# Seven products for the convolution gate zc, and a layer norm one pair sooner

## The chip, the cores and the metric

The kernel runs on one core of a Trainium2 chip. The metric is the device time of one execution in microseconds (us); lower is better. A run's time is that of its only core.

The engines: TensorE (PE) multiplies; PEld is its weight load; VectorE (DVE), ScalarE (ACT) and GpSimd (POOL) do elementwise work; SyncE (SP) issues DMA transfers. ACT and POOL issue some DMAs too. SBUF is the on-chip memory (128 partitions), PSUM holds matmul results, DRAM is the memory outside.

## The reference

One decoder layer on x of 512 tokens x 2048 channels, in float32. One combined projection by w_in (2048 x 7168) gives seven parts of 1024 columns; eight heads of 128 run causal stick-breaking attention, and a depthwise convolution of width 31 with layer norm and a pointwise product makes the other half.

```python
h = _rmsnorm(x, g_pre)
q, k, v, z_att, u, g_glu, z_conv = jnp.split(h @ w_in, IN_SPLITS, axis=-1)
y_att = _stick_breaking_attention(q, k, v) * jax.nn.silu(z_att)
# _conformer_conv: u * sigmoid(g_glu), causal conv (31 taps) + conv_b,
#                  layernorm over channels, silu, then @ w_pw2 + b_pw2
y_conv = _conformer_conv(u, g_glu, ...) * jax.nn.silu(z_conv)
y = jnp.concatenate([y_att, y_conv], axis=-1) @ w_out
x = x + _rmsnorm(y, g_post)
```

The part the change concerns is `z_conv`, called zc in the kernel: 512 x 2048 times 2048 x 1024, then silu, then a product with the pointwise output.

## The kernel before

**Arithmetic.** Each float32 operand is split in two parts, hi (rounded by ACT, line 99) and lo (the rest, subtracted by DVE, line 100), and each product is three matmuls: hi·hi, hi·lo, lo·hi (`mm3`, lines 342 to 344). One matmul has 128 x 128 stationary values and streams 512 columns.

**Projections.** `pair(c0, post, name)` computes 256 output channels: two steps, one for each half of the 2048 rows of h, each of two units of 24 matmuls, 96 in all. A step's weights are one raw block of 1 MB that SP loads, and its hi and lo; each of the three has two buffers, so the block of the next step is loaded and split while this one is multiplied. Here the weights stand still and h moves, so channels lie on partitions. `post` evicts the result; `post_zc` is a Silu on ACT into `szc` (line 755).

**Strassen's products.** v is made otherwise (`values`): h and w are seen as 2 x 2 blocks, seven products of blocks replace eight. Product q takes a form of h (h's block itself for 1, 2 and 4; a sum or difference for 5, 6, 3 and 7, made by DVE in `make_v_form` in place in the raw h) and a block of w or a sum of blocks. The sums of w are made in DRAM by POOL's DMAs: a copy (line 506), then an accumulating one (line 502). `plan_sums` lists them, and `sum_next` issues the next one, held until the last matmul that was issued. Each product is two steps (kg 0 and 1) of two units of 12 matmuls, with tokens on partitions. w_out's products at the end (`product`) do likewise, 28 steps.

**Order.** PE's order is the order of the code. The orders of DVE, ACT, POOL and SP are made by a scheduler from priorities: the splits of weights get a high one, background work (`tc.cur_priority += LATER`) a low one. The steps run: u, q, k and g pairs, v's 14 steps from step 8 on, then further u, q, k and g pairs, and then the gates `gates_a` (za) and `gates_c` (zc) in the order a0, a1, c0, a2, `n_norm`, c1, c2, c3, a3, then the pointwise product `pw`, then w_out. Attention (`attention`) advances a piece after each unit: z scores, softmax on ACT and DVE with POOL's masks (line 671), ten transposes `aT` on PE (line 715), the exponential (line 707). The convolution is 31 DVE instructions a channel tile (lines 396 and 401), issued as background. From `n_norm` the layer norm is the background: `mu_hi`, `mu_lo`, PE's `ln_mu`, squares, `var_hi`, `var_lo`, `ln_var`, an inverse root, a multiplication by DVE (line 448), a scaled Silu by ACT (line 449) into `acc`, and its split `s_hi`, `s_lo`.

Of the kernel before, what the change touches and what calls it, by code (L numbers as in the profile page):

```python
# [11 lines left out]
F32 = mybir.dt.float32  # L12
# [29 lines left out]

LATER = 300

SUMS_FROM = 20


@with_exitstack
def hybrid_layer(
# [34 lines left out]
    def t2(name, dt=F32):  # L84
        return t2p.tile([P, S], dt, tag="t2", name=name)
# [260 lines left out]
    def h_at(k, lo=0, hi=S):  # L346
        return h_hi[k // 4][:, k % 4, lo:hi], h_lo[k // 4][:, k % 4, lo:hi]
# [199 lines left out]
    def make_v_form(q):  # L547

        tt = nc.vector.tensor_tensor
        for mi in range(2):  # L550
            for jj in range(2):
                first, second = raw_h[mi, jj], raw_h[2 + mi, jj]
                f = second if q == 7 else raw_h[2 + mi, 2 + jj]
                if q == 5:
                    tt(out=f, in0=second, in1=f, op=ALU.subtract)
                elif q == 6:
                    tt(out=f, in0=f, in1=first, op=ALU.subtract)
                elif q == 3:
                    tt(out=f, in0=f, in1=raw_h[mi, 2 + jj], op=ALU.add)
                else:  # L560
                    tt(out=f, in0=first, in1=f, op=ALU.subtract)
                name = f"vf{q}_{mi}{jj}"
                if q == 6:
                    hi, lo = (as_blocks(t2(f"{name}{x}", F32R)) for x in "hl")
                elif q == 5:
                    hi = early_form(name + "h")
                    lo = (
                        as_blocks(t2(name + "l", F32R)) if (mi, jj) == (1, 1)
                        else early_form(name + "l")
                    )  # L570
                else:
                    hi, lo = early_form(name + "h"), as_blocks(t2(name + "l", F32R))
                v_form[q, mi, jj] = hi, lo
                split(hi, lo, f)

    def v_stationary(q, k, i):
        if q in (1, 2, 4):
# [172 lines left out]
    szc = {}  # L750

    def post_zc(c):
        def post(i, ps):
            szc[c + i] = t2(f"szc{c + i}")
            nc.scalar.activation(szc[c + i], ps, AF.Silu)
        return post
# [290 lines left out]
    heads(3)  # L1047
    gates_a(0)
    gates_a(1)
    gates_c(0)  # L1050
    gates_a(2)
    n_norm = len(steps)
    gates_c(1)
    gates_c(2)
    gates_c(3)
    gates_a(3)
    n_in = len(steps)
    for t in range(4):
        pointwise(t)
# [243 lines left out]
```

## Time and profile before

| | us |
|---|---|
| median of 3 runs | 867.04 (866.97 to 867.11) |
| the profiled execution | 866.65 |
| its span, first to last instruction | 864.9 |
| PE busy in it | 853.0 (3884 instructions) |
| DVE, ACT, POOL busy | 632.7, 394.0, 122.8 |
| granted TensorE clock, mean (1 is 2.4 GHz) | 0.996 |

The profile is one execution as the hardware recorded it. A matmul's record (0.39 us) is longer than the distance to the next one's start, because they overlap; so PE's cost of a matmul is read from starts, or from a window's length over its count. A wait counts only where the waiting engine is one that sets the end.

### The profile page before, as it was taken

What the parts mean: (1) busy time and instruction counts of PE and PEld (TensorE: products, weight loads), DVE (VectorE), ACT (ScalarE), POOL (GpSimd) and SP (SyncE); (2) the same over time, 40 slices, a digit from 0 to 9 for tenths busy, and PEclk for the clock granted to TensorE, in tenths of its full rate; (3) what the DMA queues carried; (4) which work ended last, traced back from release to release, by engine and by line L of the source; (5) the groups of instructions that cost most, each with busy time, mean ns of one, the idle gap of its engine ahead of it and who ended that gap; (6) DMA issues with size and microseconds to landing.
All of it is one profiled execution on the core that took longest, in us unless ns stands there. A gap on an engine that the chain in (4) does not pass through costs nothing.

```text
span 864.9 us, 9821 instructions
## 1 busy us (share of the span) xinstructions
PE 853.0 (99%) x3884; PEld 706.5 (82%) x3884; DVE 632.7 (73%) x773; ACT 394.0 (46%) x451; POOL 122.8 (14%) x154
## 2 busy tenths in 40 slices
PE   9999999999999999999999999999999999999995
PEld 6888888888888888888888887888888888888884
DVE  5799989767499797979969697244543776458775
ACT  5785222565524333445432454235732346455542
POOL 0111110010022112312110414041001000000031
PEclk9999999999999999999999999999999999999998
DMA  8798996455965945487448843785223255557783
GB/s 325 230 291 197 254 267 159 153 189 200 334 155 138 243 146 194 100 194 191 150 150 190 179 166 120 218 195 146 97 98 98 98 171 218 195 195 259 288 275 103
DMA packets 87046, 163.58 MB, mean 189 GB/s; under 512 B 3014, under 2 KB 52434, under 8 KB 83224
## 3 DMA queue, kind: packets, MB, share of 16 engines
q1 hardware_dynamic: 69824, 110.12, 37.1%
q0 software_dynamic: 16864, 52.43, 26.5%
q8 instruction: 30, 0.49, 0.2%
q10 hardware_dynamic: 312, 0.40, 0.1%
q14 instruction: 16, 0.13, 0.1%
HBM read 158.75 MB, written 54.53 MB: 247 GB/s over the span
## 4 chain that ended last, share of the span: by engine, by line
PE 91%; DVE 6%; ACT 2%; issue 1%; DMA 1%; POOL 0%; DVEq 0%; SPq 0%; ACTq 0%; POOLq 0%
PE u L342 3%; PE k L342 3%; PE q L342 3%; PE q L344 3%; PE u L344 3%; PE q L343 3%; PE a L940 3%; PE u L343 3%; PE a L942 3%; PE k L343 3%; PE a L941 3%; PE k L344 3%; PE zc L344 3%; PE zc L342 3%; PE zc L343 3%; DVE acc L401 2%
## 5 line engine op out<-in xcount | busy, mean ns | idle before, releaser
L401 DVE SCALAR_TENSOR_TENSOR acc<-hg,vec,acc 128x512 f32<-128x512 f32 x240 | 181.1, 755 | 7.2
L100 DVE TENSOR_TENSOR l_w<-r_w,h_w 128x2048 fp32r<-128x2048 f32 x28 | 64.0, 2290 | 42.5 <-ACT h_w L99 42.3
L99 ACT ACTIVATE h_w<-r_w 128x2048 fp32r<-128x2048 f32 x28 | 53.5, 1915 | 43.7 <-DMA r_w<-ws 11.1
L344 PE MATMUL zc<-h_hi,l_zc 128*128 128x512 f32 x128 | 49.9, 390 | 0.7 <-DVE l_zc L100 0.7
L342 PE MATMUL u<-h_hi,h_u 128*128 128x512 f32 x128 | 50.1, 392 | 0.0
L342 PE MATMUL q<-h_hi,h_q 128*128 128x512 f32 x128 | 50.1, 392 | 0.0
L342 PE MATMUL k<-h_hi,h_k 128*128 128x512 f32 x128 | 50.1, 391 | 0.0
L342 PE MATMUL za<-h_hi,h_za 128*128 128x512 f32 x128 | 50.0, 390 | 0.0
L342 PE MATMUL zc<-h_hi,h_zc 128*128 128x512 f32 x128 | 49.9, 390 | 0.0
L344 PE MATMUL q<-h_hi,l_q 128*128 128x512 f32 x128 | 49.9, 390 | 0.0
L344 PE MATMUL u<-h_hi,l_u 128*128 128x512 f32 x128 | 49.9, 390 | 0.0
L344 PE MATMUL za<-h_hi,l_za 128*128 128x512 f32 x128 | 49.8, 389 | 0.0
L344 PE MATMUL k<-h_hi,l_k 128*128 128x512 f32 x128 | 49.8, 389 | 0.0
L343 PE MATMUL u<-h_lo,h_u 128*128 128x512 f32 x128 | 49.8, 389 | 0.0
L343 PE MATMUL q<-h_lo,h_q 128*128 128x512 f32 x128 | 49.8, 389 | 0.0
L343 PE MATMUL za<-h_lo,h_za 128*128 128x512 f32 x128 | 49.8, 389 | 0.0
L343 PE MATMUL k<-h_lo,h_k 128*128 128x512 f32 x128 | 49.8, 389 | 0.0
L343 PE MATMUL zc<-h_lo,h_zc 128*128 128x512 f32 x128 | 49.8, 389 | 0.0
L940 PE MATMUL a<-h_w,f_hi 128*128 128x512 f32 x128 | 49.8, 389 | 0.0
L941 PE MATMUL a<-l_w,f_hi 128*128 128x512 f32 x128 | 49.8, 389 | 0.0
L942 PE MATMUL a<-h_w,f_lo 128*128 128x512 f32 x128 | 49.8, 389 | 0.0
L100 DVE TENSOR_TENSOR l_v<-r_v,h_v 128x2048 fp32r<-128x2048 f32 x14 | 32.1, 2290 | 17.1 <-ACT h_v L99 17.1
(339 smaller groups left out, 2132.2 us busy)
## 6 DMA issues: line engine op xcount, KB each, us to landing
ws<-in_w_out_dram POOLq DMA_DIRECT2D x24, 1024.0 KB, 9.4
r_w<-ws SPq DMA_DIRECT2D x16, 1024.0 KB
vs<-in_w_in_dram POOLq DMA_DIRECT2D x12, 1024.0 KB, 9.5
r_w<-in_w_out_dram SPq DMA_DIRECT2D x12, 1024.0 KB
r_u<-in_w_in_dram SPq DMA_DIRECT2D x8, 1024.0 KB
r_q<-in_w_in_dram SPq DMA_DIRECT2D x8, 1024.0 KB
r_k<-in_w_in_dram SPq DMA_DIRECT2D x8, 1024.0 KB
r_v<-vs SPq DMA_DIRECT2D x8, 1024.0 KB
```

Source lines behind the costliest of these rows:

```text
L99: nc.scalar.activation(hi, src, AF.Copy)
L100: nc.vector.tensor_tensor(out=lo, in0=src, in1=f32(hi), op=ALU.subtract)
L342: nc.tensor.matmul(ps, wh, ah, start=first, stop=False)
L343: nc.tensor.matmul(ps, wh, al, start=False, stop=False)
L344: latest[0] = nc.tensor.matmul(ps, wl, ah, start=False, stop=last).ins
L401: bgq.append(lambda j=j: nc.vector.scalar_tensor_tensor(out=acc, in0=hg[:, j : j + S], scalar=vec[:, ct, j : j + 1], in1=acc, op0=ALU.mult ...
L940: nc.tensor.matmul(ps, fh[:, kk, ts], hi[:, k, :], start=st, stop=False, skip_group_check=True)
L941: nc.tensor.matmul(ps, fh[:, kk, ts], lo[:, k, :], start=False, stop=False, skip_group_check=True)
L942: nc.tensor.matmul(ps, fl[:, kk, ts], hi[:, k, :], start=False, stop=en, skip_group_check=True)
```

## The change

zc leaves the pairs and is made as v is, by seven products of 2 x 2 blocks (`gates_c()`, 14 steps), in one stage after all za pairs. Five things come with it.

- The forms of h that v's stage makes are stored to DRAM (`kept_form`, 16 stores of 256 KB in ACT's queue), loaded again by SP into the buffers of h's parts as these come free (`load_form`, 4 loads of 1 MB) and split again by ACT and DVE (`split_form`).
- Sixteen more DMAs of 1 MB make the sums of w (`z_sum`), alternating with those for w_out. The sums run at 1.5 a step from step 20 to the z stage, none in it, and go on after it.
- Results are tokens by channels (`z_done`: 8 copies on ACT, 8 combinations on DVE). `turn_z` transposes them back, 32 times 128 x 128 on PE, behind the 24 matmuls of each of the first two pointwise units, and ACT's Silu reads from the transposed PSUM tile.
- The steps run a0, a1, a2, `n_norm` (step 48 in place of 50), a3, the 14 z steps, pw, w_out: 96 steps in place of 90.
- After `n_norm` the background's priority is low (`background(2, LATER)`).

```diff
@@ make_v_form
                 v_form[q, mi, jj] = hi, lo
                 split(hi, lo, f)
+                nc.scalar.dma_start(as_blocks(kept_form[q][:, 2 * mi + jj, :]), f)
@@
+    Z_ORDER = (1, 2, 4, 5, 6, 3, 7)
+    z_sum, z_sumq = plan_sums("zs", (5, 6, 4, 7), 1, z_w)
+    def load_form(q):
+        hi = act8.tile([P, 4, S], F32R, tag="act", name=f"zf_hi{q}")
+        lo = act8.tile([P, 4, S], F32R, tag="act", name=f"zf_lo{q}")
+        z_form[q] = hi, lo
+        nc.sync.dma_start(f32(lo), kept_form[q])
+    def split_form(q):
+        hi, lo = z_form[q]
+        tc.cur_priority += LATER
+        for n in range(2):
+            ms = slice(2 * n, 2 * n + 2)
+            split(hi[:, ms], lo[:, ms], f32(lo[:, ms]))
+        tc.cur_priority -= LATER
...
+    def z_load(q, kg):
+        form = {(2, 1): 5, (4, 1): 6, (5, 1): 3, (6, 1): 7}.get((q, kg))
+        if form:
+            load_form(form)
...
+            nc.sync.dma_start(raw, z_w(*PLAIN[q], 0, kg) if q in PLAIN else z_sum[q, 0, kg])
+            split(hi, lo, raw)
+        form = {(4, 0): 5, (5, 0): 6, (6, 1): 3, (3, 1): 7}.get((q, kg))
+        if form:
+            split_form(form)
+        return hi, lo
...
+    def z_done(q, i):
...
+        if q == 1:
+            z_nat[i, 0] = kept("z11_")
+        elif q == 2:
+            tt(out=z_nat[i, 0], in0=ps, in1=z_nat[i, 0], op=ALU.add)
+        elif q == 4:
+            z_nat[2 + i, 0] = kept("z21_")
...
+        else:
+            tt(out=z_nat[2 + i, 0], in0=ps, in1=z_nat[2 + i, 0], op=ALU.add)
+            tt(out=z_nat[2 + i, 1], in0=z_nat[2 + i, 1], in1=ps, op=ALU.subtract)
+    def turn_z(count):
+        for _ in range(min(count, len(turns))):
+            c = turns.popleft()
+            ps = op2.tile([P, S], F32, tag="o2", name=f"zT{c}")
+            for m in range(NT):
+                cs = slice(c % 4 * P, (c % 4 + 1) * P)
+                nc.tensor.transpose(ps[:, m * P : (m + 1) * P], z_nat[m, c // 4][:, cs], ident)
+            szc[c] = t2(f"szc{c}")
+            nc.scalar.activation(szc[c], ps, AF.Silu)
@@ pointwise
                     mm3(ps, (hi[:, k, cs], lo[:, k, cs]), (s_hi[k], s_lo[k]), k == 0, k == CT - 1)
+                turn_z(4)
                 yc = szc[c]
@@ the order of the steps
     gates_a(0)
     gates_a(1)
-    gates_c(0)
     gates_a(2)
     n_norm = len(steps)
-    gates_c(1)
-    gates_c(2)
-    gates_c(3)
     gates_a(3)
+    n_zc = len(steps)
+    gates_c()
@@ the loop over the steps
-        if n >= SUMS_FROM:
-            sum_next(sumq)
+        if SUMS_FROM <= n < n_zc - 1 or n >= n_in:
+            due += SUMS_A_STEP
...
+            if due >= 1:
+                sum_next(sumq)
+                due -= 1
...
-                background(2, 0)
+                background(2, LATER)
```

Three places where the order of instructions changes. The first is ACT around head 7's exponential (`t3_7`), which waits for DVE and which POOL's masks and PE's transposes `aT7` follow; `h_za21` and the like are roundings of weights. Before:

```order
L745 ACTIVATE sz2_3964<-za1_0_3825 128x512
L707 ACT_TABLE_LOAD
L707 ACTIVATE t3_7_3908<-t3_7_3908 128x1280
L99 ACTIVATE h_zc01_4005<-r_zc01_4004 128x2048
L745 ACT_TABLE_LOAD
L745 ACTIVATE sz3_3995<-za1_1_3854 128x512
```

After:

```order
L748 ACTIVATE sz2_4001<-za1_0_3863 128x512
L99 ACTIVATE h_za21_4042<-r_za21_4041 128x2048
L710 ACT_TABLE_LOAD
L710 ACTIVATE t3_7_3947<-t3_7_3947 128x1280
L748 ACT_TABLE_LOAD
L748 ACTIVATE sz3_4033<-za1_1_3893 128x512
```

The rounding of the second half's weights has moved from behind the exponential to ahead of it.

The second is DVE at the same head: scans (line 702 before, 705 after), the addition into `t3_7` that the exponential reads (706, 709), and convolution steps of the last tile (`acc7`). Before:

```order
L694 SCALAR_TENSOR_TENSOR t1_7_3907<-z7_3894,t1_7_3907 128x1280
L401 SCALAR_TENSOR_TENSOR acc7_3325<-hg7_3322,vec_126,acc7_3325 128x512
L702 SCALAR_TENSOR_TENSOR t3_7_3908<-t1_7_3907 128x128
L702 SCALAR_TENSOR_TENSOR t3_7_3908<-t1_7_3907 128x256
L702 SCALAR_TENSOR_TENSOR t3_7_3908<-t1_7_3907 128x384
L702 SCALAR_TENSOR_TENSOR t3_7_3908<-t1_7_3907 128x512
L401 SCALAR_TENSOR_TENSOR acc7_3325<-hg7_3322,vec_126,acc7_3325 128x512
L706 TENSOR_TENSOR t3_7_3908<-z7_3894,t3_7_3908 128x1280
L401 SCALAR_TENSOR_TENSOR acc7_3325<-hg7_3322,vec_126,acc7_3325 128x512 x2
```

After:

```order
L697 SCALAR_TENSOR_TENSOR t1_7_3946<-z7_3933,t1_7_3946 128x1280
L401 SCALAR_TENSOR_TENSOR acc7_3358<-hg7_3355,vec_126,acc7_3358 128x512 x4
L705 SCALAR_TENSOR_TENSOR t3_7_3947<-t1_7_3946 128x128
L705 SCALAR_TENSOR_TENSOR t3_7_3947<-t1_7_3946 128x256
L705 SCALAR_TENSOR_TENSOR t3_7_3947<-t1_7_3946 128x384
L705 SCALAR_TENSOR_TENSOR t3_7_3947<-t1_7_3946 128x512
L709 TENSOR_TENSOR t3_7_3947<-z7_3933,t3_7_3947 128x1280
L100 TENSOR_TENSOR l_za21_4043<-r_za21_4041,h_za21_4042 128x2048
```

All four remaining convolution steps stand ahead of the scans, and the subtraction for the next weights stands right behind the addition.

The third is ACT where the norm's Silus (line 449) and the splits `s_hi` fall among the roundings of weights (`h_zc30` before, `h_z40` after) and, after, of forms (`zf_hi5`). Before:

```order
L99 ACTIVATE h_zc30_4519<-r_zc30_4518 128x2048
L449 ACT_TABLE_LOAD
L449 ACTIVATE acc0_862<-acc0_862,vec_126 128x512
L449 ACTIVATE acc1_896<-acc1_896,vec_126 128x512
L99 ACTIVATE s_hi0_4644<-acc0_862 128x512
L449 ACTIVATE acc2_2019<-acc2_2019,vec_126 128x512
L755 ACTIVATE szc4_4548<-zc2_0_4442 128x512
L449 ACTIVATE acc3_2051<-acc3_2051,vec_126 128x512
```

After:

```order
L821 COPY z11_1_4458<-za_1_4371 128x512
L99 ACTIVATE zf_hi5_4464<-zf_lo5_4465 128x1024
L449 ACT_TABLE_LOAD
L449 ACTIVATE acc0_866<-acc0_866,vec_126 128x512
L99 ACTIVATE zf_hi5_4464<-zf_lo5_4465 128x1024
L99 ACTIVATE h_z40_4512<-r_z40_4511 128x2048
L449 ACTIVATE acc1_900<-acc1_900,vec_126 128x512
L449 ACTIVATE acc2_2039<-acc2_2039,vec_126 128x512
L449 ACTIVATE acc3_2072<-acc3_2072,vec_126 128x512
L449 ACTIVATE acc4_2582<-acc4_2582,vec_126 128x512
L99 ACTIVATE h_z41_4567<-r_z41_4566 128x2048
```

Roundings of forms and copies of products have come between, and a rounding of weights is due every 24 matmuls in place of every 48.

## Rows read from the trace of the kernel before

**Rows 1.** The page: each engine's busy time; GB/s in 40 slices of the span.

```profile
PE 853.0 (99%) x3884; PEld 706.5 (82%) x3884; DVE 632.7 (73%) x773; ACT 394.0 (46%) x451; POOL 122.8 (14%) x154
GB/s 325 230 291 197 254 267 159 153 189 200 334 155 138 243 146 194 100 194 191 150 150 190 179 166 120 218 195 146 97 98 98 98 171 218 195 195 259 288 275 103
```

**Rows 2.** Waits of PE: line, releaser, us in total, times, longest.

```profile
PE zc L344 <- DVE l_zc L100: 0.7, 1, 0.7
```

**Rows 3.** Windows (v, zc, products): us; busy (instructions) by engine; PEclk, DMA share, GB/s.

```profile
140.00:216.00 76.00, 76.00 (x336) 62.60 (x335) 57.35 (x55) 37.99 (x40) 3.26 (x3) 1.00 0.53 176
...
576.00:660.00 84.00, 84.00 (x372) 69.50 (x371) 41.34 (x49) 42.62 (x54) 9.37 (x6) 1.00 0.44 123
...
716.00:760.00 44.00, 44.00 (x195) 36.42 (x195) 23.72 (x19) 24.05 (x27) 0.00 (x0) 1.00 0.57 204
```

**Rows 4.** Timeline of PE from 535: start, us, instruction, idle before it and its releaser.

```profile
535.17 1.25 PE L715 MATMUL aT<-ident,t 128*128 128x128 f32 x10
536.18 0.48 PE L342 MATMUL zc<-h_hi,h_zc 128*128 128x512 f32 x1
536.50 0.40 PE L343 MATMUL zc<-h_lo,h_zc 128*128 128x512 f32 x1
537.58 0.50 PE L344 MATMUL zc<-h_hi,l_zc 128*128 128x512 f32 x1 [0.69 <-DVE l_zc L100]
```

**Rows 5.** Groups by line: busy us, mean ns, then idle before and releasers.

```profile
L715 PE MATMUL aT<-ident,t 128*128 128x128 f32 x80 | 10.0, 272 | 0.0
L99 ACT ACTIVATE h_v<-r_v 128x2048 fp32r<-128x2048 f32 x14 | 26.8, 1916 | 29.6 <-PE g L343 13.1 <-PE va L636 10.1 <-PE vc L636 3.1
L100 DVE TENSOR_TENSOR l_v<-r_v,h_v 128x2048 fp32r<-128x2048 f32 x14 | 32.1, 2290 | 17.1 <-ACT h_v L99 17.1
```

**Rows 6.** Timelines of DVE, ACT and POOL around head 7's exponential.

```profile
523.22 0.74 DVE L401 SCALAR_TENSOR_TENSOR acc<-hg,vec,acc 128x512 f32<-128x512 f32 x1
528.89 1.48 DVE L706 TENSOR_TENSOR t<-z,t 128x1280 f32<-128x1280 f32 x1
...
531.74 1.27 ACT L707 ACTIVATE t<-t 128x1280 f32<-128x1280 f32 x1
532.92 1.90 ACT L99 ACTIVATE h_zc<-r_zc 128x2048 fp32r<-128x2048 f32 x1
...
533.09 1.03 POOL L671 TENSOR_SCALAR_AFFINE_SELECT t<-t 128x128 f32<-128x128 f32 x4 [5.20 <-ACT t L707]
...
534.85 2.68 DVE L100 TENSOR_TENSOR l_zc<-r_zc,h_zc 128x2048 fp32r<-128x2048 f32 x1 [3.04 <-ACT h_zc L99]
```

**Rows 7.** Timelines of DVE and PE: the norm's means.

```profile
552.26 0.68 DVE L100 TENSOR_TENSOR mu_lo<-ln_sum,mu_hi 128x512 fp32r<-128x512 f32 x1
577.26 0.39 PE L424 MATMUL ln_mu<-mu_hi,mean_w 128*128 128x512 f32 x1
590.64 0.69 DVE L100 TENSOR_TENSOR var_lo<-ln_sq,var_hi 128x512 fp32r<-128x512 f32 x1 [0.70 <-ACT var_hi L99]
599.51 0.39 PE L424 MATMUL ln_var<-var_hi,mean_w 128*128 128x512 f32 x1
```

**Rows 8.** Timeline of ACT: the norm's last part.

```profile
607.35 1.28 ACT L449 ACT_TABLE_LOAD   x1
610.07 0.62 ACT L99 ACTIVATE s_hi<-acc 128x512 fp32r<-128x512 f32 x1
612.82 3.63 ACT L449 ACTIVATE acc<-acc,vec 128x512 f32<-128x512 f32 x5
```

**Rows 9.** Timelines of DVE and PE: a split and its first use, early.

```profile
86.43 2.29 DVE L100 TENSOR_TENSOR l_q<-r_q,h_q 128x2048 fp32r<-128x2048 f32 x1 [0.31 <-ACT h_q L99]
95.34 0.39 PE L342 MATMUL q<-h_hi,h_q 128*128 128x512 f32 x1
```

**Rows 10.** DMA issues of POOL: times, KB each, median us from issue to landing.

```profile
ws<-in_w_out_dram POOLq DMA_DIRECT2D x24, 1024.0 KB, 9.4
ws<-ws POOLq DMA_DIRECT2D x8, 5.5
```

More of the change, by code (lines that the diff above doesn't have):

```diff
@@ L43 @@
 LATER = 300
-SUMS_FROM = 20
+SUMS_FROM, SUMS_A_STEP = 20, 1.5
 @with_exitstack
@@ L539, in hybrid_layer @@
     v_form, v_ps, v_part = {}, {}, {}
+    kept_form = {q: dram.tile([P, 4, S], F32, name=f"kept{q}") for q in (5, 6, 3, 7)}
     def as_blocks(t):
@@ L748, in post_za, with z_w @@
         return post
[L750 to L756, printed above, removed]
+    Z_ORDER = (1, 2, 4, 5, 6, 3, 7)
+    szc, z_form, z_ps, z_nat, turns = {}, {}, {}, {}, deque()
+    def z_w(r, c, p, kg):
+        rows_ = slice((r * 2 + kg) * S, (r * 2 + kg + 1) * S)
+        return w_in[rows_, C_ZC + c * S : C_ZC + (c + 1) * S].rearrange("(k p) c -> p k c", p=P)
+    z_sum, z_sumq = plan_sums("zs", (5, 6, 4, 7), 1, z_w)
@@ new lines, in load_form, with z_stationary @@
+    def load_form(q):
[10 more added lines that the diff above has]
+        tc.cur_priority -= LATER
+    def z_stationary(q, k, i):
+        if q in (1, 2, 4):
+            t = (2 if q == 4 else 0) + i
+            return h_at(k if q == 1 else 8 + k, t * P, (t + 1) * P)
+        hi, lo = z_form[q]
+        cs = slice(k % 4 * P, (k % 4 + 1) * P)
+        return hi[:, 2 * i + k // 4, cs], lo[:, 2 * i + k // 4, cs]
@@ new lines, in z_load @@
+    def z_load(q, kg):
+        form = {(2, 1): 5, (4, 1): 6, (5, 1): 3, (6, 1): 7}.get((q, kg))
+        if form:
+            load_form(form)
+        name = f"z{q}{kg}"
+        ahead = min(2000, tc.cur_priority - floor[0])
+        with tc.high_priority(offset=ahead):
+            raw = raws.tile([P, 4, S], F32, tag="raw", name=f"r_{name}")
+            hi = his.tile([P, 4, S], F32R, tag="hi", name=f"h_{name}")
+            lo = los.tile([P, 4, S], F32R, tag="lo", name=f"l_{name}")
+            nc.sync.dma_start(raw, z_w(*PLAIN[q], 0, kg) if q in PLAIN else z_sum[q, 0, kg])
[4 more added lines that the diff above has]
+        return hi, lo
@@ new lines, in z_bank, with kept @@
+    def z_bank(q, i):
+        if q == 1 and i == 0:
+            for n in range(2):
+                z_ps["b", n] = mm(f"zb{n}")
+            for n in range(2):
+                z_ps["a", n] = mm(f"za_{n}")
+        if q in (2, 4):
+            z_ps["c", i] = op2.tile([P, S], F32, tag="o2", name=f"zc{q}_{i}")
+        z_ps[q, i] = z_ps[{2: "c", 4: "c", 5: "b", 3: "b"}.get(q, "a"), i]
+    def z_done(q, i):
+        ps = z_ps[q, i]
+        tt = nc.vector.tensor_tensor
+        def kept(name):
+            t = t2(f"{name}{i}")
+            nc.scalar.copy(t, ps)
+            return t
+        if q == 1:
[4 more added lines that the diff above has]
+            z_nat[2 + i, 0] = kept("z21_")
+        elif q == 5:
+            z_nat[2 + i, 1] = kept("z22_")
+        elif q == 6:
+            z_nat[i, 1] = kept("z12_")
+        elif q == 3:
+            tt(out=z_nat[i, 1], in0=ps, in1=z_nat[i, 1], op=ALU.subtract)
+        else:
+            tt(out=z_nat[2 + i, 0], in0=ps, in1=z_nat[2 + i, 0], op=ALU.add)
+            tt(out=z_nat[2 + i, 1], in0=z_nat[2 + i, 1], in1=ps, op=ALU.subtract)
+            if i == 1:
+                turns.extend(range(CT))
@@ new lines, in turn_z, with z_unit, go @@
+    def turn_z(count):
[7 more added lines that the diff above has]
+            nc.scalar.activation(szc[c], ps, AF.Silu)
+    def z_unit(q, kg, i):
+        def go(w):
+            hi, lo = w
+            if kg == 0:
+                z_bank(q, i)
+            ps = z_ps[q, i]
+            for k in range(4):
+                ah, al = z_stationary(q, kg * 4 + k, i)
+                st, en = q in (1, 2, 4, 5) and kg + k == 0, kg == 1 and k == 3
+                nc.tensor.matmul(ps, ah, hi[:, k, :], start=st, stop=False, skip_group_check=True)
+                nc.tensor.matmul(ps, ah, lo[:, k, :], start=False, stop=False, skip_group_check=True)
+                latest[0] = nc.tensor.matmul(
+                    ps, al, hi[:, k, :], start=False, stop=en, skip_group_check=True
+                ).ins
+            if kg == 1:
+                z_done(q, i)
+        return go
@@ L759, in pointwise, with gates_c @@
+    def gates_c():
+        for q in Z_ORDER:
+            for kg in range(2):
+                steps.append(Step(
+                    lambda q=q, kg=kg: z_load(q, kg), [z_unit(q, kg, 0), z_unit(q, kg, 1)]
+                ))
     def pointwise(t):
@@ L836, in w_block @@
         return w_out[rows, cols].rearrange("(k p) c -> p k c", p=P)
-    w_sum, sumq = plan_sums("ws", (5, 6, 4, 7), 2, w_block)
+    w_sum, w_sumq = plan_sums("ws", (5, 6, 7, 4), 2, w_block)
+    sumq = deque()
+    while w_sumq:
+        sumq.extend(q.popleft() for q in (z_sumq, w_sumq) if q)
     turn = [0]
@@ L1024, in gates_a @@
         pair(C_ZA + t * 256, post_za(2 * t), f"za{t}")
-    def gates_c(t):
-        pair(C_ZC + t * 256, post_zc(2 * t), f"zc{t}")
     def gate_in(t):
@@ L1232, in background @@
                 tc.cur_priority -= later
-    units_done = 0
+    units_done, due = 0, 0
     for n, step in enumerate(steps):
```

## The prediction, made before the changed kernel ran

> **What bounds the kernel now.** I read the page's busy line first: TensorE (PE) is busy for 853.0 of 864.9 us [rows 1]. Then the waits: the only one of PE's that lies within the change's reach is a zc matmul that waits 0.7 us for VectorE's (DVE's) `l_zc` [rows 2]. Then the stages: in v's stage, in the zc stage and in the products PE is busy for the whole of each window, at a granted clock of 1.00, which is the upper level, 2.4 GHz, while ScalarE (ACT) and DVE have a quarter to a half of their time free [rows 3]. So the time is the number of PE's passes times the time of one, plus what PE is made to wait. A change pays here only by taking passes away, and it can lose only by making PE wait. The sum is made against the profiled execution, 866.65 us, of which 1.75 lie around the span; the median of the three runs is 867.04, so 0.39 is added at the end.
>
> **Passes removed.** zc by four pairs is 4 x 96 = 384 matmuls of 512 columns. Seven products x 2 halves of the rows x 2 units x 12 are 336. v's stage is just that count in just that form: 336 matmuls fill 76.00 us, 0.226 each [rows 3]. Removed: 48 x 0.2262 = 10.9 us.
>
> **Passes added.** The products come out with tokens on partitions, so 32 transposes of 128x128 stand behind the first pointwise units. Ten such transposes of a head's `aT` start at 535.17 and the next matmul starts at 536.18: 1.01 us, 0.10 each; with a little for the change of shape I take 0.11, so 32 cost 3.5 us [rows 4]. The ends are 0.10 (3.2) and the mean length of one record, 0.272 (8.7), if none overlapped the next [rows 5]. They wait for DVE's last combinations of product 7, but 24 pointwise matmuls (5.4 us) stand between the two in PE's order, against four DVE instructions of 0.7; no wait is expected. The eight Silus on ACT that follow replace eight that were there. The other combinations and copies (8 copies, 8 additions) lie on ACT and DVE, beside PE.
>
> The skill has a price of its own for a transpose. The Trainium skill, "TensorE: Matmul & The Clock Gate", section "Part 4: PE-mode transpose", puts a 128x128 transpose in a kernel at about 275 ns. That agrees with the record's length here (272) but not with the spacing of starts (0.10); by it the 32 would be an estimated 8.8 us and the sum 5.3 higher.
>
> **The stall that goes.** The half zc01 begins late: between 536.50 and 537.58 lie 1.08 us where 0.23 are normal, so 0.85 are lost [rows 4]. Its cause is an order, not a load: ACT ran `h_zc` at 532.92, behind head 7's exponential at 531.74, which had waited for DVE's `t` (528.89 + 1.48); so `l_zc` ran from 534.85 to 537.53 [rows 6]. In the changed order `h_za21` stands ahead of that exponential. `l_za21` then follows DVE's `t` at once, done near 534 against a need at 536.7. The 0.85 goes.
>
> What is late next there is the head itself. Four convolution steps, not one, now stand ahead of head 7's scans, and none between the scans and `t`: three more of 0.74 ahead and one fewer between put `t` 1.5 us later. GpSimd's (POOL's) masks ended at 534.12, the transposes started at 535.17: 1.05 of slack [rows 4, 6]. Expected: 0.4 us of wait, between 0 and 1.5.
>
> **The norm a pair sooner.** `ln_mu` stands 96 matmuls earlier in PE's order: 577.26 - 21.7 = 555.5. `mu_lo` was done at 552.94 and nothing new stands ahead of it, so 2.6 us of margin remain. `ln_var` stands 86 passes (19.5 us) behind `ln_mu` in place of 98 (22.25); the work between them took from 577.26 to 591.33, 14.1 us, so 5.4 remain [rows 7]. Cost 0, up to 1.
>
> **The z stage's splits.** Each of 14 steps is 24 matmuls, 24 x 0.2262 = 5.43 us. For each, ACT rounds (1.92) and then DVE subtracts (2.29) a 1 MB block, 4.2 in a row, two buffers [rows 5]; 1.2 us of slack per step. v's stage bore this, but there ACT was busy for 38.0 and DVE for 57.4 of 76 us [rows 3]. Here the norm's end and the forms fall in the same stretch. In five steps of z2 to z5 (27.2 us) ACT has five roundings (9.6), eight `L449` (3.63 / 5 = 0.73 each, 5.8), a table load (1.28), eight `s_hi` (0.62, 5.0), three halves of a form (1.0 each, an estimate from half of 1.92) and two copies (0.6 each, like `s_hi`): 25.9 of 27.2 [rows 5, 8]. Four steps reach PE's need within 0.3 us either way when I lay these durations along the changed order. I take 0.8 us lost. The ends are 0 and 5.5: if each of the five splits stands behind two `L449` on ACT (1.46) and one `L448` or `s_lo` of 0.7 on DVE, it is 2.2 late against 1.2 of slack, and 1.0 to 1.1 a step is lost.
>
> **Stores, loads and sums.** Sixteen 256 KB stores join ACT's queue in q's and v's stages, ahead of roundings of `h_q`, and DVE, which makes form 6 in place, must wait until form 5's stores have read their tiles. `l_q` was done at 88.7, PE needed it at 95.34 [rows 9]. Even a landing as slow as POOL's 1 MB (9.4) [rows 10] puts it near 93. Cost 0, up to 2. Four form loads of 1 MB stand among the raw loads in SyncE's (SP's) queue; each is issued about 4 us away from its neighbours. Cost 0; the other end is a rival. The sums now run at 1.5 a step, 16 MB more in all, and pause in the z stage. Each is an issue on POOL ahead of some head's masks; they are released by PE's units, as before. Cost 0, up to 1.
>
> **Sum.** 866.65 - 10.9 + 3.5 - 0.85 + 0.4 + 0.8 = 859.6; with 0.39, **860.0 us**.
>
> **Rivals.**
> A. The splits pace the z stage: all of the 5.5 above instead of 0.8, 864.7. For it: ACT at 95% through five steps. Against it: the scheduler puts the weights' roundings ahead of the norm's work wherever both are ready.
> B. Slower: the form loads hold up the raw loads behind them. A raw load has about 6.6 us, from its buffer's release to its rounding (5.43 a step, plus the 1.2 of slack). If a form stands right ahead of it and a 1 MB load takes t, it is 2t - 6.6 late, four times. At t = 9.4, as POOL's 1 MB loads took, that is 12.2 x 4 = 49 us; at 5.5, POOL's other row, 4.4 x 4 = 17.6, so 877.6 [rows 10]. The net gain of 7.0 is used up at t = 4.2, from where the change loses. Against it: the fastest slice of the page moved 334 GB/s, at which 1.05 MB take 3.1 us, two 6.3 [rows 1]; the products moved 204 GB/s with a 1 MB load in each 24 matmuls and PE waited for none [rows 3]; the z stage needs 18.9 MB in 76 us, 248 GB/s, with the sums paused, and the forms are issued some 4 us from their neighbours.
> The Trainium skill, "DMA: Bandwidth & Descriptors", section "Anatomy of one DMA — SWDGE (gpsimd) path", gives 2.0 us plus the bytes at 436 GB/s for a POOL load: an estimate of 4.4 us for 1 MB, by which B would cost 8.8 and the time be 868.8. Its two rows here are longer, 9.4 and 5.5, with other loads on the engines at the time.
> C. The transposes cost their record's whole length: 32 x 0.163 = 5.2 more, 865.2. Against it: the ten at 535.17.
> D. The change does not get the norm sooner: the last convolution or `mu_lo` slips past 555.5 and PE waits in order at `ln_mu`, with every matmul behind it. Each us late costs one; with a slip of 5 us against 2.6 of margin, 862.4.
>
> **How the numbers follow.** Forecast 0.58 (858.2 to 862.5), A 0.15, B 0.08, C 0.08, D 0.11. The range goes from 858.0 (no wait at all is 866.65 - 10.9 + 3.2 - 0.85 + 0.39 = 858.5, and half a us for the profiled run's own scatter) to 866.0, which takes in A, C and D. A difference of 0.2%, 1.7 us, is about what can be told from none: 865.3 to 868.8 is the same. Of A, C and D about a third lies over 865.3: same 0.11. Slower is B alone with a remainder of mishaps on both, 0.08. Faster 0.81.
>
> **What would show it.** Right: PE with 336 z matmuls at 0.226 and 32 transposes over 3.2 to 3.8 us; no wait for `l_z` over 0.5 us; the wait at 537 gone. A shows as PE waits on DVE `l_z` between z2 and z5, B as ACT's `h_z` waiting for a load with PE behind it, C as 0.27 from start to start, D as a PE wait at `ln_mu` or `ln_var`. I would be wrong altogether if PE's clock fell in the z stage or if new waits appeared ahead of it, in the stages where the stores and the faster sums run.

## The result and the profile after

The changed kernel takes 860.26 us in the median of four runs (859.57 to 861.26), the kernel before 867.00 beside it: ratio 0.9923, 95% interval 0.9906 to 0.9941. It is faster by 6.7 us; the forecast was 7.0 us, to 860.0, in a range of 858.0 to 866.0. Five further runs of the same kernel, made later, have a median of 861.65 (under The spread, below). The profiled run took 860.66, its span 858.7, so 1.96 lie around it. From the page (it answers [rows 1]):

```profile
PE 846.6 (99%) x3868; PEld 701.9 (82%) x3868; DVE 660.7 (77%) x795; ACT 416.3 (48%) x473; POOL 139.4 (16%) x170
```

When PE reached each place, from the timelines of PE of both kernels (us from the span's start):

| PE starts | before | after | after - before |
|---|---|---|---|
| u, the first pair | 61.74 | 62.05 | +0.31 |
| v's stage | 149.74 | 150.13 | +0.39 |
| u behind v's stage | 226.29 | 228.53 | +2.24 |
| head 7's transposes | 535.17 | 537.30 | +2.13 |
| pointwise | 659.84 | 650.12 | -9.72 |
| w_out's products | 703.36 | 697.18 | -6.18 |

So the gain is made between 535 and 660, 11.85 us; 3.54 are given back in the pointwise stage, as expected; and 1.85 are lost in v's stage, which the change was not to touch in PE's work. The other 0.39 lie ahead of it: over all the traces below the first transposes `gT` start between 59.77 and 60.96, with no order in it, so that is scatter of the start.

The waits of PE [rows 2]: the one for `l_zc` is gone, and there is a new one, in v's stage.

```profile
PE idle L1244 <- POOL mean_w L134: 1.8, 1, 1.8
PE va L638 <- DVE l_v L100: 1.2, 1, 1.2
```

PE's timeline there; and where the transposes stand in the pointwise stage, and head 7's transposes [rows 4]:

```profile
155.57 0.39 PE L637 MATMUL va<-h_v,h_hi 128*128 128x512 f32 x1
157.12 0.50 PE L638 MATMUL va<-l_v,h_hi 128*128 128x512 f32 x1 [1.16 <-DVE l_v L100]
...
537.07 0.39 PE L344 MATMUL za<-h_hi,l_za 128*128 128x512 f32 x1
537.30 1.25 PE L718 MATMUL aT<-ident,t 128*128 128x128 f32 x10
538.30 0.48 PE L342 MATMUL za<-h_hi,h_za 128*128 128x512 f32 x1
...
655.57 1.91 PE L849 MATMUL zT<-ident,z 128*128 128x128 f32 x16
657.23 0.48 PE L342 MATMUL pw<-s_hi,h_pw 128*128 128x512 f32 x1
```

From 155.57 to the next start are 1.55 us instead of 0.23: 1.32 of the 1.85 lost. Sixteen transposes take 1.66 us from start to start, 0.104 each. `aT` follows the matmul ahead of it by 0.23, so it waits for nothing.

The z stage as one window of all engines, from its first matmul to the first pointwise one, and below it v's stage of the kernel before, from v's first matmul to the next one of u (us; busy of PE, PEld, DVE, ACT and POOL with instructions; PEclk, DMA share, GB/s) [rows 3]:

```profile
573.47:650.12 76.65, 76.65 (x339) 63.45 (x338) 59.62 (x57) 57.12 (x61) 1.49 (x1) 1.00 0.65 233
149.74:226.29 76.55, 76.55 (x338) 62.91 (x336) 54.77 (x49) 41.72 (x42) 4.54 (x4) 1.00 0.58 200
```

And the tightest place in it, in the timelines of DVE and PE [rows 5]:

```profile
593.44 2.29 DVE L100 TENSOR_TENSOR l_z<-r_z,h_z 128x2048 fp32r<-128x2048 f32 x1
...
595.73 0.39 PE L862 MATMUL zc<-h_z,h_hi 128*128 128x512 f32 x1
595.95 0.39 PE L863 MATMUL zc<-l_z,h_hi 128*128 128x512 f32 x1
```

In the z stage 338 matmuls start, its 336 and two of the norm, with PE busy throughout: 0.2268 each and no wait. (The window named v in [rows 3], 140 to 216, begins 9.7 us ahead of v's stage; that it too counts 336 is chance.) But ACT is busy for 57.1 us in the z stage where v's stage before has 41.7, and the `l_z` of the fifth step ended at 595.73, with its first use at 595.95: 0.22 us of margin.

**Where v's stage lost it.** DVE and ACT in q's and k's pairs, and DVE at v's second step (this is where [rows 9] were read):

```profile
82.66 0.69 DVE L559 TENSOR_TENSOR xw<-xw,whole 128x512 f32<-128x512 f32 x1 [1.50 <-DMA kept<-xw]
...
85.46 0.69 DVE L559 TENSOR_TENSOR xw<-xw,whole 128x512 f32<-128x512 f32 x1 [1.50 <-DMA kept<-xw]
...
101.41 0.33 ACTq L577 DMA_DIRECT2D kept<-xw  x1
101.83 1.92 ACT L99 ACTIVATE h_k<-r_k 128x2048 fp32r<-128x2048 f32 x1 [11.22 <-DMA kept<-xw]
...
103.78 2.29 DVE L100 TENSOR_TENSOR l_k<-r_k,h_k 128x2048 fp32r<-128x2048 f32 x1 [2.31 <-ACT h_k L99]
...
125.84 0.68 DVE L100 TENSOR_TENSOR k_lo<-k,k_hi 128x512 fp32r<-128x512 f32 x1
...
154.78 2.28 DVE L100 TENSOR_TENSOR l_v<-r_v,h_v 128x2048 fp32r<-128x2048 f32 x1
```

The same in the kernel before, with PE's first use of that `l_v`:

```profile
97.97 2.28 DVE L100 TENSOR_TENSOR l_k<-r_k,h_k 128x2048 fp32r<-128x2048 f32 x1
...
119.02 2.29 DVE L100 TENSOR_TENSOR l_g<-r_g,h_g 128x2048 fp32r<-128x2048 f32 x1 [1.57 <-ACT h_g L99]
123.37 0.69 DVE L100 TENSOR_TENSOR k_lo<-k,k_hi 128x512 fp32r<-128x512 f32 x1 [2.06 <-ACT k_hi L99]
...
152.31 2.28 DVE L100 TENSOR_TENSOR l_v<-r_v,h_v 128x2048 fp32r<-128x2048 f32 x1
155.40 0.39 PE L635 MATMUL va<-l_v,h_hi 128*128 128x512 f32 x1
```

Form 6 is made in place over form 5, and DVE waits twice for form 5's stores. A store of form 7 stands in ACT's queue until 101.41, and behind it the rounding `h_k`, at 95.36 before, which starts at 101.83. So `l_k`, at 97.97 before, comes at 103.78, 5.8 us late. Two gaps that DVE had before, 1.57 us ahead of `l_g` and 2.06 ahead of `k_lo`, are used up, and `k_lo` is still 2.47 late. From 115.45 to behind v's second step DVE has work without a gap, most of it convolution steps, so it cannot catch up: `l_v` is 2.47 late too, and its end at 157.06 is what PE waits for. In the kernel before it ended at 154.59 and PE used it at 155.40, a margin of 0.81; PE itself is 0.39 late, so 2.47 - 0.81 - 0.39 = 1.27 should be lost, and 1.32 are. At a later step it is still late, and two starts of PE lie 0.79 apart in place of 0.45:

```profile
171.49 2.28 DVE L100 TENSOR_TENSOR l_v<-r_v,h_v 128x2048 fp32r<-128x2048 f32 x1
...
173.38 0.39 PE L637 MATMUL vb<-h_v,vf_00h 128*128 128x512 f32 x1
173.83 0.50 PE L638 MATMUL vb<-l_v,vf_00h 128*128 128x512 f32 x1
174.17 0.39 PE L639 MATMUL vb<-h_v,vf_00l 128*128 128x512 f32 x1
```

That is 0.34 more, 1.66 in all; 0.19 stay spread over the rest of the stage.

### The profile page after: what moved, and what is told of

It is laid out like the page before. It is cut to its first block, busy times and chain, and to the rows that moved or that the text cites. A ratio compares the mean times of both kernels' runs of the same rounds, so it can differ in the third digit from the quotient of the medians.

```text
span 858.7 us, 9932 instructions
## 1 busy us (share of the span) xinstructions
PE 846.6 (99%) x3868; PEld 701.9 (82%) x3868; DVE 660.7 (77%) x795; ACT 416.3 (48%) x473; POOL 139.4 (16%) x170
## 4 chain that ended last, share of the span: by engine, by line
PE 84%; DVE 8%; DMA 4%; ACT 2%; issue 1%; POOL 0%; DVEq 0%; ACTq 0%; POOLq 0%
PE za L343 3%; PE za L342 3%; PE za L344 3%; PE a L1067 3%; PE a L1065 3%; PE a L1066 3%; PE u L344 3%; PE u L343 3%; PE u L342 3%; DVE acc L401 3%; PE q L344 3%; PE k L344 3%; PE q L342 3%; PE k L343 3%; PE k L342 3%; PE q L343 3%
## 5 line engine op out<-in xcount | busy, mean ns | idle before, releaser
L100 DVE TENSOR_TENSOR l_z<-r_z,h_z 128x2048 fp32r<-128x2048 f32 x14 | 32.0, 2288 | 16.2 <-ACT h_z L99 16.2
L674 POOL TENSOR_SCALAR_AFFINE_SELECT t<-t 128x128 f32<-128x128 f32 x64 | 35.2, 585 | 53.6 <-ACT t L710 29.5
L99 ACT ACTIVATE h_v<-r_v 128x2048 fp32r<-128x2048 f32 x14 | 26.8, 1916 | 29.4 <-PE g L343 13.2
```

The source lines that it names most:

```text
L674: nc.gpsimd.affine_select(out=blk, in_=blk, compare_op=ALU.is_gt, fill=0.0, base=0, pattern=[[-1, P]], channel_multiplier=1,)
```

## The experiments

The theory: the passes, the transposes and the stall are as forecast, and the loss in v's stage comes from the stores, by way of DVE's backlog. Times are medians; the kernel before took 866.8 to 867.1 beside each of them.

### The stores taken out of the change, and put alone into the kernel before

`e1_no_stores`:

```diff
-                nc.scalar.dma_start(as_blocks(kept_form[q][:, 2 * mi + jj, :]), f)
...
-        nc.sync.dma_start(f32(lo), kept_form[q])
+        nc.sync.dma_start(f32(lo), v_sum[4 if q == 3 else q, 0, 0])
```

> The changed kernel without the sixteen stores of the forms; the four form loads of 1 MB read a finished sum of v's weights instead (same size and layout), so four of the seven products of zc use wrong forms. Theory (the stores make DVE and ACT late in q's and k's pairs, and the v stage pays): the wait of PE for l_v at 155.57 (1.32 us) and the 0.2 to 0.5 us behind it go, v's stage takes 76.2 us instead of about 77.7, time 858.3 to 858.8, and the runs lie closer together than the 1.7 us of the changed kernel. Rival (the wait is only the new order of DVE, or comes from the sums): the wait stays, 860.3. Rival (the z stage sits on its edge and the earlier start takes it up): 859.5 or more.

858.79 (858.71 to 858.88). PE's only wait left is the one at the start. 1.47 us less, and the runs within 0.17 of each other. PE takes 76.5 us from v's first matmul to the next one of u, as in the kernel before (76.55), where the changed kernel takes 78.4. Head 7 in this trace, for the account below:

```profile
531.99 1.28 ACT L709 ACTIVATE t<-t 128x1280 f32<-128x1280 f32 x1
533.34 1.02 POOL L673 TENSOR_SCALAR_AFFINE_SELECT t<-t 128x128 f32<-128x128 f32 x4 [5.64 <-ACT t L709]
535.43 1.25 PE L717 MATMUL aT<-ident,t 128*128 128x128 f32 x10
```

`b1_stores_alone`, the kernel before with:

```diff
+    kept_form = {q: dram.tile([P, 4, S], F32, name=f"kept{q}") for q in (5, 6, 3, 7)}
...
                 split(hi, lo, f)
+                nc.scalar.dma_start(as_blocks(kept_form[q][:, 2 * mi + jj, :]), f)
```

> The kernel before with nothing added but the sixteen stores of the forms, which nobody reads. Theory (the stores make DVE late through q's and k's pairs, and v's second step pays): a wait of PE for l_v near 155 of 1 to 1.5 us, 868.3 to 869.0 against 866.97, and a wider spread of the runs. Rival (the wait in the changed kernel came from another of its parts): 866.8 to 867.2.

868.40 (867.67 to 872.53), 1.35 more than the 867.05 beside it, with the same wait as in the changed kernel, and the old one still there:

```profile
PE va L638 <- DVE l_v L100: 1.2, 1, 1.2
PE zc L344 <- DVE l_zc L100: 0.7, 1, 0.7
```

The stores cost 1.4 to 1.5 us, by themselves, in either kernel (1.9 in the changed one, if its median over all nine runs is taken, 860.66).

### Which of their waits it is

`e3_stores_from_hi` takes away DVE's waits, not ACT's:

```diff
-                nc.scalar.dma_start(as_blocks(kept_form[q][:, 2 * mi + jj, :]), f)
+                nc.scalar.dma_start(as_blocks(kept_form[q][:, 2 * mi + jj, :]), f32(hi) if q == 5 else f)
```

> The changed kernel with form 5's four stores reading the rounded part hi, which nobody overwrites, instead of the raw form, which DVE overwrites to make form 6; so product 5 of zc loses its form's lo part. Same number of stores, same bytes, same queue. Theory (ACT's queue): DVE's two waits of 1.5 us at L559 go, but h_k still starts after 100 and the wait for l_v stays at 1 us or more: 860.0 to 860.5. Rival (the in-place waits): DVE is 3 us earlier and the wait for l_v goes: 858.4 to 858.9.

859.38 (859.17 to 860.25): between the two. DVE's waits at L559 are gone, ACT still stood 12.2 us at a store, and PE's wait for `l_v` is 0.3 us. So the waits in place are worth about 0.9 of the 1.5 us. The other 0.6 are left to ACT's queue and to the stores' traffic; this run does not part the two.

`e2_stores_by_pool` takes the stores out of ACT's queue:

```diff
-                nc.scalar.dma_start(as_blocks(kept_form[q][:, 2 * mi + jj, :]), f)
+                nc.gpsimd.dma_start(as_blocks(kept_form[q][:, 2 * mi + jj, :]), f)
```

> The changed kernel with the same sixteen stores issued by POOL instead of ACT. Theory (ACT's queue is what makes it late: it stood 11.2 us at the store of form 7 and h_k behind it): the rounding h_k starts near 91 instead of 101.8, no wait for l_v, 858.4 to 858.9. Rival (DVE's waits for the stores of form 5, two of 1.5 us, make it late): POOL's stores land later than ACT's, DVE waits 3 us or more, 860.3 or more, up to 863. Rival (the traffic itself, which makes raw loads late): unchanged, 860.3.

864.27 (863.23 to 865.26). The second possibility held, and cost more than its range: issued behind the sums of v's weights, form 5's stores land late, and DVE waits 8.6 us in place. The third, that the traffic alone costs it, would have left the time as it was. PE then waits already in q's and k's pairs. Waits of DVE from 60 to 130, then of PE:

```profile
DVE xw L559 <- DMA kept<-xw: 8.6, 1, 8.6
...
PE k L344 <- DVE l_k L100: 1.9, 2, 1.6
PE q L344 <- DVE l_q L100: 1.1, 1, 1.1
```

`i1_stores_in_v` holds all stores until their step in v's stage and writes form 6 elsewhere:

```diff
-                f = second if q == 7 else raw_h[2 + mi, 2 + jj]
+                last = raw_h[2 + mi, 2 + jj]
+                f = {5: last, 6: first, 3: last, 7: second}[q]
...
-                    tt(out=f, in0=f, in1=first, op=ALU.subtract)
+                    tt(out=second, in0=first, in1=second, op=ALU.subtract)
+                    tt(out=f, in0=last, in1=first, op=ALU.subtract)
...
-                nc.scalar.dma_start(as_blocks(kept_form[q][:, 2 * mi + jj, :]), f)
+                tc.add_manual_dep(
+                    nc.scalar.dma_start(as_blocks(kept_form[q][:, 2 * mi + jj, :]), f).ins,
+                    latest[0].name,
...
```

(`first` and `second` are the two blocks of h that form 7 is the difference of; the line that writes `second` takes that difference early. Form 6 goes over `first`, and form 3 over form 5.)

> The changed kernel with two edits in v's stage: each store of a form is held until PE has reached the step ahead of the one whose weights are loaded with it, and form 6 is written over another block of h (form 7's difference is taken first), so that DVE need not wait for form 5's stores. Theory (the stores cost 1.5 us only because they stand in ACT's queue in q's and k's pairs and because form 6 was made in place): no wait of PE for l_v, 858.5 to 859.0, as without the stores (858.79), and runs within 0.4 us of each other. Rival (the stores' traffic costs by itself, wherever it stands): 859.5 to 860.3. Rival (ACT's stores now delay v's roundings): a wait in v's stage, 860 or more.

861.63 (861.07 to 862.89): not better than the change, and outside the theory's range. The edit only moved the wait, as the next run confirms: form 3's addition, which now overwrites form 5, had been placed ahead of v's stage, and there DVE waits for the held stores, right ahead of the same `l_v`. DVE's timeline, then PE's wait:

```profile
146.75 0.69 DVE L563 TENSOR_TENSOR xw<-whole,xw 128x512 f32<-128x512 f32 x1 [2.53 <-DMA kept<-xw]
```

```profile
PE va L643 <- DVE l_v L100: 1.9, 1, 1.9
```

`i5_no_wait_in_place` writes form 3 over form 6 instead and holds only form 7's stores:

```diff
-                f = second if q == 7 else raw_h[2 + mi, 2 + jj]
+                last = raw_h[2 + mi, 2 + jj]
+                f = {5: last, 6: first, 3: first, 7: second}[q]
...
+                store = nc.scalar.dma_start(as_blocks(kept_form[q][:, 2 * mi + jj, :]), f)
+                if q == 7:
+                    tc.add_manual_dep(
+                        store.ins, latest[0].name,
...
```

> The changed kernel with form 6 (and later form 3) written over another block of h, so that DVE need not wait for form 5's stores, and with only form 7's four stores held until PE has reached their step in v's stage; the other stores stay where the changed kernel has them. Theory (two causes, each worth a part: DVE's two waits of 1.5 us, and the store of form 7 at which ACT's queue stood 11.2 us): DVE is some 3 us earlier at v's stage, h_k starts near 91 to 95, no wait for l_v over 0.3 us: 858.6 to 859.4. Rival (moving stores only moves the wait, as in i1_stores_in_v, where form 3's addition waited 2.5 us for form 5's held stores): 860.3 or more.

859.03 (858.63 to 859.42), ratio to before 0.9905 (0.9888 to 0.9921). It is the fastest complete kernel here, and all four runs lie below the nine of the changed kernel. PE's wait for `l_v` is 0.3 us. `h_k` came later than forecast, though, at 96.57: with no store ahead of them the roundings now wait for their raw loads (`r_k` 9.6 us, `r_q` 8.2). In `e1_no_stores`, as in the kernel before, no rounding between 60 and 130 waits for a load; from 80 to 100 that trace has 261 GB/s and this one 321. So it is the stores that make the loads late. Only form 7's have left this stretch, and the time is 0.24 us over `e1_no_stores`. The 0.35 between `e3_stores_from_hi` and this run would then be ACT's queue, but their ranges overlap, so that part is argued and not shown.

### The other terms

`e4_order_alone`, the kernel before with:

```diff
-    gates_c(0)
     gates_a(2)
     n_norm = len(steps)
+    gates_a(3)
+    gates_c(0)
     gates_c(1)
     gates_c(2)
     gates_c(3)
-    gates_a(3)
```

> The kernel before with its steps in the changed order and nothing else: za0, za1, za2, then the norm, za3, and the four pairs of zc. It keeps 384 matmuls. Theory: ln_mu comes 96 matmuls sooner, near 555, with no wait; in this order of ACT head 7's exponential still stands ahead of the rounding of the second half's weights, so the wait of 0.7 us near 537 stays: 866.8 to 867.2. Rival (the stall belonged to the zc pair and goes with it): 866.0 to 866.3. Rival (the norm is not ready a pair sooner): a wait at ln_mu, 868 or more.

866.93 (866.62 to 867.71), ratio 0.9998 (0.9989 to 1.0007). The norm's matmuls wait for nothing; the stall at 536.5 stays, now in za:

```profile
PE za L344 <- DVE l_za L100: 0.7, 1, 0.7
```

So the stall does not belong to the zc pair. It stays where ACT's order stays (here the rounding `h_za` ran at 532.90, behind head 7's exponential at 531.72) and goes where that rounding stands ahead of the exponential, as in the changed kernel (526.38 and 533.04).

`z1_transposes_twice`, on `i1_stores_in_v`:

```diff
-                nc.tensor.transpose(ps[:, m * P : (m + 1) * P], z_nat[m, c // 4][:, cs], ident)
+                for _ in range(2):
+                    nc.tensor.transpose(ps[:, m * P : (m + 1) * P], z_nat[m, c // 4][:, cs], ident)
```

> As i1_stores_in_v, with each of the 32 transposes issued twice into the same place, 64 in all. Theory (0.104 us each, as their starts show): 3.3 us longer than i1_stores_in_v, 862.0 to 862.4 if that is 858.8. Rival (each costs its record's 0.272 us): 8.7 longer, 867.5.

865.45, 3.8 more than `i1_stores_in_v`. In the trace 32 in a row take 3.41 us, 0.107 each, where 16 took 1.66, and the pointwise stage is 3.49 longer:

```profile
657.66 3.66 PE L855 MATMUL zT<-ident,z 128*128 128x128 f32 x32
661.07 0.48 PE L342 MATMUL pw<-s_hi,h_pw 128*128 128x512 f32 x1
```

Rival C is out: a transpose costs PE the distance of starts, not its record.

`z3_form_rounded_twice`, on `i1_stores_in_v`:

```diff
+            nc.scalar.activation(hi[:, ms], f32(lo[:, ms]), AF.Copy)
             split(hi[:, ms], lo[:, ms], f32(lo[:, ms]))
```

> As i1_stores_in_v, with ACT's rounding of each form's half done twice (8 more roundings of 1.0 us, the same values). Theory (the z stage sits on its edge: in the changed kernel l_z of the fifth step was ready 0.23 us before PE needed it): the two extra roundings of form 5 make the fifth step 1.0 to 1.8 us late, and up to as much again behind it: 1 to 3.5 us longer than i1_stores_in_v. Rival (ACT's idle time in the stage, a quarter, takes them up): 0 to 0.3 us longer.

862.79 (861.13 to 863.78) against 861.63 (861.07 to 862.89): 1.2 more, but the ranges overlap, so the times do not part the two possibilities. The traces say more: PE's z stage is 0.65 us longer (77.30 against 76.65), between the two. Its only new wait is 0.26 us for `l_z` at 630; the order was made anew, and the second half of form 5 moved behind the roundings it would have delayed. So eight us more of ACT did not come through the fifth step, which had its 0.23 of margin again.

### The form loads: rival B

`z2_form_loads_twice`, on `i1_stores_in_v`:

```diff
+        nc.sync.dma_start(f32(hi), kept_form[q])
         nc.sync.dma_start(f32(lo), kept_form[q])
```

> As i1_stores_in_v, with each of the four form loads issued twice (once into the hi tile, which the rounding then overwrites): 8 MB instead of 4 in SP's queue in the z stage. Theory (a 1 MB load takes about 3 us there and the raw loads have that to spare): 0 to 1 us longer than i1_stores_in_v. Rival B of the prediction (each load pushes the raw load behind it): 4 x 3 = 12 us longer, less what the window absorbs, so 4 to 12.

865.76, 4.1 more, inside rival B's range and still not by its mechanism: in the z stage no rounding waits for a load in this trace. The order is another one. Seven `L448`, a combination and a form's half now stand ahead of the fifth step's `l_z` on DVE, where `i1_stores_in_v` has six `L448`, and PE waits for it. DVE's timeline, then PE's wait:

```profile
590.57 3.69 DVE L448 TENSOR_TENSOR acc<-acc,ln_y 128x512 f32<-128x512 f32 x6
...
595.38 1.22 DVE L100 TENSOR_TENSOR zf_lo<-zf_lo,zf_hi 128x1024 fp32r<-128x1024 f32 x1
596.52 2.28 DVE L100 TENSOR_TENSOR l_z<-r_z,h_z 128x2048 fp32r<-128x2048 f32 x1
```

```profile
PE zc L869 <- DVE l_z L100: 2.0, 1, 2.0
```

That is rival A, at its place, in a neighbour of the changed kernel. The wait is half of the 4.0 us by which the z stage grew; most of the rest is the granted clock, which fell behind it (0.52 and 0.63 in the two windows from 600 to 604).

`i7_sums_in_z_stage`, on `i5_no_wait_in_place`:

```diff
-        if SUMS_FROM <= n < n_zc - 1 or n >= n_in:
+        if n >= SUMS_FROM:
```

> As i5_no_wait_in_place, with the sums not paused in the z stage: 1.5 of them a step there too, each 1 MB read and 1 MB written by POOL's DMAs, beside the weights and the forms. Theory (the raw loads have time to spare there: with the form loads doubled no rounding waited for a load): up to 0.5 us more than 859.0. Rival B (the stage's loads are near what the DMA engines give): roundings h_z wait for raw loads and PE for l_z, 862 to 880.

870.89 (869.37 to 872.74), 11.9 more, and 4 more than the kernel before. Here the theory falls, and rival B holds as this run put it: the loads come late and PE waits behind them. It is not quite the B of the prediction, where the form loads hold up the raw loads; here the sums do. POOL's DMAs, at 9.4 us to landing in the changed kernel, take 20.2, and the loads beside them are late. Waits of ACT from 570 to 670, and of PE:

```profile
ACT h_z L99 <- DMA r_z<-zs: 4.6, 2, 3.2
...
PE zc L869 <- DVE l_z L100: 4.1, 3, 1.8
PE zc L868 <- ACT h_z L99: 2.0, 1, 2.0
```

The DMA issues from 574 to 650 (count, KB each, median us from issue to landing):

```profile
ws<-in_w_out_dram POOLq DMA_DIRECT2D x4, 1024.0 KB, 20.2
```

So the pause of the sums, which the prediction names only in passing among the points against rival B, is what keeps the loads in time.

### The spread

`a2_changed_again` is the changed kernel, unedited.

> The changed kernel once more, for its spread. Theory (the wait for l_v near 155 differs from run to run with what the DMA queues do, and after a wait of about 2 us the clock is at its lower level for some 3.4 us, as in z1_transposes_twice and e2_stores_by_pool): runs between 859.3 and 863, where i5_no_wait_in_place stays within 0.8. Rival (the spread of 1.7 us was chance): all within 0.5 of 860.2.

861.65 (859.89 to 862.16). With the four above, nine runs lie between 859.57 and 862.16, where `e1_no_stores` has 0.17 and `i5_no_wait_in_place` 0.8. In this trace, of the run that took 862.16, there is a second wait, in k's pair, besides the one in v's stage:

```profile
PE k L344 <- DVE l_k L100: 1.2, 1, 1.2
PE va L638 <- DVE l_v L100: 1.1, 1, 1.1
```

ACT again stood at a store of form 7, until 102.11, and the second `h_k` waited 9.95 us for its raw load, so that the second `l_k` ended at 119.12. In the profiled run of the result it ended at 117.74, 0.12 ahead of its use: the changed kernel has an edge here too. From u's first product to v's stage PE takes 89.63 us in this trace and 88.08 in the other, which covers the difference of the two runs (1.50). So what the stores cost differs from run to run. That this is all of the spread is not shown: the other seven runs left no trace, and the kernel before, which has no such stores, spread by 1.9 over 16 runs. Nor is it shown that a fallen clock has a part in it; in the two traces of the changed kernel the clock is at 1.00 behind the waits.

## Why the prediction was right

By its steps, against the profiled run (forecast 859.6, measured 860.66):

- **Passes removed**, -10.9, and **the stall**, -0.85: together 11.75, and 11.85 were gained between head 7 and the pointwise stage. Right. The price of a pass was read from a window that is not v's stage (140 to 216); v's own stage, 336 matmuls in 76.55 us with 0.4 of small waits in it, gives the same. `e4_order_alone` fits the stall being ACT's order, as said.
- **Transposes**, +3.5: 3.3 from start to start (0.104 each), and 3.54 with the change of shape behind them. Right, and `z1_transposes_twice` confirms the price. The Trainium skill, "TensorE: Matmul & The Clock Gate", section "Part 4: PE-mode transpose", has about 275 ns for one in a kernel. Here they start 0.104 us apart behind one another, so as a cost on PE's path that figure does not hold, as both kernels' traces show.
- **Head 7's wait**, +0.4: nothing, and the delay it rests on did not come. The exponential ran at 533.04, 1.30 us later than before, but PE was 2.13 late there. In `e1_no_stores`, where nothing is late, the exponential ran at 531.99, 0.25 later than before, and PE came 0.26 later: the masks were done at 534.36 and the transposes started at 535.43, 1.07 of slack against 1.05 before. The four convolution steps do stand ahead of the scans, but DVE came to the instruction in front of them (L694 before, L696 here) at 518.65 in place of 521.82, mostly because at head 6 the rounding of weights had moved ahead of the exponential too, and DVE's wait for it had shrunk from 3.21 to 0.55 us. The steps were counted right; the start that they were counted from was the old one.
- **The norm**: `mu_lo` ended at 555.21, its matmul was at 556.90; `var_lo` at 570.69 for a matmul at 576.43. No wait, so rival D did not happen. Right; 1.7 of margin at the first, not 2.6.
- **The splits**, +0.8: nothing in this order, by 0.22 us. The reading of the edge was nearly right (four steps within 0.3 of PE's need; the trace has one at 0.22 and three at 0.5 to 0.6, and ACT busy for 26.7 of the 27.2 us from 582.2, where 25.9 were counted); a small change of the order (`z2_form_loads_twice`) makes it a wait of 2 us, 4 with the clock that falls behind it.
- **The stores**, 0, up to 2: 1.5 to 1.85. This is the step that failed. It followed the lateness only to the next use, `l_q`, with 6.6 us of margin, and stopped there; that far it was right (`l_q` was done at 92.93, where 93 was worked out). What was late on DVE was carried on, less the gaps that DVE had on the way, since it has work to do up to v's second step, and there the kernel before had 0.8 us: `l_v` ended at 154.59, PE used it at 155.40. Two further ways had no price in it: that ACT stands at a store with the rounding `h_k` behind it, and that the raw loads come late beside the stores. The prediction had named new waits ahead of the z stage, where the stores run, as a sign of being wrong altogether. That sign came, with 1.16 us; the sum held because the cost was small.
- **Rivals**: A and B did not happen; but both stand close by, A one order away and late loads one pause away. C is refuted by the starts. Of B, the Trainium skill, "DMA: Bandwidth & Descriptors", section "Anatomy of one DMA — SWDGE (gpsimd) path", gives 2.0 us plus the bytes at 436 GB/s, an estimate of 4.4 us for 1 MB issued by POOL; here it was 9.4, and 20.2 in `i7_sums_in_z_stage`, so the traces disagree where other loads are in flight.

The sum was right to 1.1 us, and that to some part by luck: 1.2 us of waits that did not come stood against 1.85 that did. So was the closeness of 860.26 to 860.0: the five further runs have 861.65.

## What to carry to other kernels

When a new instruction makes an engine late, follow the lateness down that engine's queue, less each gap on the way, and not only to the next use: here DVE was 5.8 us late at 104, still 2.5 at 155 after two gaps, and the margin to look up was that of the last step ahead of the next gap. A store that reads a buffer which is updated in place makes the update wait for the landing (two waits of 1.5 us here); write the update elsewhere. And where the bound is PE with its loads just in time, the traffic that is paused there belongs to the change as much as the work that is moved in.

## What the runs showed of the hardware

After some waits of 1.6 to 2.0 us PE's clock fell to its lower level for a while. In `z1_transposes_twice`, PE waited 1.99 us, ran five matmuls with starts 0.23 to 0.34 apart, and then its starts lay 0.40 to 0.43 apart. PE's timeline, from the wait to where they widen:

```profile
157.59 0.50 PE L643 MATMUL va<-l_v,h_hi 128*128 128x512 f32 x1 [1.99 <-DVE l_v L100]
...
158.85 0.60 PE L642 MATMUL va<-h_v,h_hi 128*128 128x512 f32 x1
159.25 0.63 PE L643 MATMUL va<-l_v,h_hi 128*128 128x512 f32 x1
```

The windows of all engines (the granted clock is the first number behind POOL's count):

```profile
158.00:160.00 2.00, 2.00 (x8) 1.63 (x7) 1.89 (x4) 0.00 (x0) 0.00 (x0) 0.72 0.55 128
160.00:162.00 2.00, 2.00 (x6) 1.51 (x6) 2.00 (x2) 0.38 (x1) 0.12 (x1) 0.50 0.99 377
```

0.50 is the lower of the two levels, 1.2 GHz. v's first product, 48 matmuls, took 14.80 us there and 13.06 in `i1_stores_in_v`, whose wait at the same place was 1.88 and whose clock stayed at 1.00: the fall cost some 1.6 us, about as much as the wait. The waits of 1.16 us in the changed kernel brought none. The same is seen in `e2_stores_by_pool` (after 1.60 us), `z2_form_loads_twice` (after 2.0 us at zc, but not after 2.1 in v's stage) and `i7_sums_in_z_stage` (after 1.96 and 1.83 close together, but not after a later 1.82); in `z3_form_rounded_twice` a wait of 1.97 brought none. What decides it stays open.

ACT's queue stood 11.2 to 12.2 us at one store of form 7, whose data had long been ready (in the changed kernel DVE had made form 7 by 88.55, and the store left at 101.41). For 6.5 of these 11.2 us ACT had work to do: `h_k` ran at 95.36 before. The profile puts the wait down to the landing of another DMA; which one was not tried.
